# First chunk of the down product: its operands split during the gate/up units, stored as hi and lo, and loaded as whole pages

## The chip, the cores and the metric

One Trainium2 chip, one of its cores. The metric is the device time of one execution in microseconds (us); below, PE, DVE, ACT, POOL and SP are the core's tensor, vector, scalar, GpSimd and sync engines. SP and POOL issue transfers (DMAs).

## The reference, cut to what matters

```python
D_MODEL, SEQ, DEPTH = 1024, 1024, 2
D_FF = ((8 * D_MODEL // 3 + 255) // 256) * 256        # 2816
def swiglu(h, w_gate, w_up, w_down):
    return (jax.nn.silu(h @ w_gate) * (h @ w_up)) @ w_down

def reference(x, ...):
    for i in range(DEPTH):
        h = rms_norm(x, mix_norm[i])
        if i % 2 == 0:
            x = x + short_conv_mixer(h, ...)
        else:
            x = x + dilated_attention_mixer(h, ...)
        h = rms_norm(x, ffn_norm[i])
        x = x + swiglu(h, w_gate[i], w_up[i], w_down[i])
    return rms_norm(x, final_norm)
```

All of it is float32. The change lies in `swiglu`, which runs twice.

## The kernel before, in words

**Products in two parts.** Each float32 operand is split into a high part (ACT copies it to the float32r type) and a low part (DVE subtracts the high part from it). A product is three matmuls: high by high, high by low, low by high (L564 to L566). Weights are split by the helper `split` (lines L139 and L140), activations by `hi` (L556 and L557).

**Winograd.** A product of two by two blocks is made with seven products instead of eight, numbered 1 to 7 and taken in the order 1, 2, 6, 5, 7, 3, 4 (`WINOGRAD`). Of the FFN there are 22 *units*: an even one is a gate, the odd one after it an up of the same two tiles of hidden rows, and the two make a *pair*. From unit 6 on (`SIMPLE`) the products of a pair are interleaved, and products 2 and 4 of a unit are split once more by the same scheme into seven small ones (`DEEPER` + i, 128x256 in PSUM). A step is written (unit, product). DVE combines weights (`combo`), adds up the products in SBUF (`part`, lines L574 and L643, which empty PE's PSUM banks) and multiplies gate by up (L1175). `store` then makes the seven combinations that the down product needs from a pair (`sum`), and POOL stores each to DRAM as `parts[q, m]`, 128x512 (L728, L748), for pair q and product m.

**The down product** takes nine pairs in three chunks of three (`FFN_CHUNK`). For each chunk and each m, `feed` loads three tiles `hin` of 128x512 from `parts` by SP (L763, 256 KB each), and one step later splits them into pages `b`, where a page is 128x1024 and holds high and low side by side: 21 splits per chunk, 126 in all. `down(c, n)` makes the products and adds each result to the residual tile X (L787), which also frees the PSUM bank. The weights of the down product (`raw`, 128x768) and the residual tiles (`x`, loaded back from `spill`) come by the same queue of SP.

**The order of the work.** Each engine takes its instructions in the order in which the code is run. `products` walks the list of steps and calls `filled(n)` in each one, and there the first chunk's feeder makes a step: the first time at (21, `DEEPER`+6), the last small steps of the last unit. So the first chunk's splits lie partly at the end of the units and partly in `down(0, 0)`. A buffer (a `page` or a `half_page`) comes from a pool of slots; the next instruction that writes to a slot waits for the last user of it.

Of the kernel before, what the change touches and what calls it, by code (L numbers as in the profile page):

```python
# [10 lines left out]
F32 = mybir.dt.float32  # L11
F32R = mybir.dt.float32r
# [5 lines left out]
S = 1024  # L18
# [11 lines left out]
WINOGRAD = (1, 2, 6, 5, 7, 3, 4)  # L30
DEEP, DEEPER = (2, 4), 10
SIMPLE = 6
# [63 lines left out]
def trunk(ctx: ExitStack, tc: tile.TileContext, x, gains_in, cwi, ck, cwo, wqkv, wo, relb,  # L96
          wg, wu, wd, oneh, ident, out):
    nc = tc.nc
# [3 lines left out]
    dram = ctx.enter_context(tc.tile_pool(name="dram", bufs=1, space=DRAM))  # L102
    ctx.enter_context(tc.manual_schedule())

    def page(name, dt=F32):
        return pages.tile([128, 1024], dt, name=name, tag="page", bufs=PAGES)
# [3 lines left out]
    def half_page(name, dt=F32):  # L110
        return scope["pool"].tile([128, 512], dt, name=name, tag="half", bufs=scope["halves"])
# [4 lines left out]
    def half(h):  # L116
        return slice(h * HALF, (h + 1) * HALF)
# [11 lines left out]
    def split(src, dst=None, eng=nc.vector):  # L129

        w = src.shape[1]
        if dst is None:
            if w <= HALF:
                t = page("w", F32R)
                dst = t[:, :w], t[:, HALF:HALF + w]
            else:
                dst = page("w_hi", F32R)[:, :w], page("w_lo", F32R)[:, :w]
        hi, lo = dst
        nc.scalar.activation(hi, src, AF.Copy)  # L139
        eng.tensor_tensor(out=lo, in0=src, in1=hi, op=ALU.subtract)  # L140
        return hi, lo
# [4 lines left out]
    ops, made, op_state = [], {}, [0, 0]  # L146
    combos, raw_base, sums_of = {}, {}, {}

    def load_raw(upto):
        while raw_state[0] < min(upto + 1, len(raw_src)):  # L150
            i = raw_state[0]
            raw_tile[i] = page("raw")
            nc.sync.dma_start(raw_tile[i][:, :raw_src[i].shape[1]], raw_src[i])
            raw_state[0] += 1
# [5 lines left out]
    def ensure(upto):  # L160
        while op_state[0] < min(upto + 1, len(ops)):
            key = ops[op_state[0] + 1][0] if op_state[0] + 1 < len(ops) else None
            if key in sums_of:
                sums_of.pop(key)()
            made[op_state[0]] = ops[op_state[0]][1]()
            op_state[0] += 1
# [91 lines left out]
    def unit_order(nu, conv):  # L258

        order = [(0, 1), (1, 1), (0, 2), (1, 2), (2, 1), (2, 2), (3, 1)]  # L260
        if conv:
            order += [(3, 2), (4, 1), (4, 2)] + [(u, m) for m in (6, 7, 5, 4, 3) for u in (0, 1)]
            order += [(2, 6), (2, 5), (2, 7)]
        else:
            order += [(3, 2)] + [(u, m) for m in (6, 7, 4, 5, 3) for u in (0, 1)] + [(2, 6), (2, 5), (2, 7)]
        order += [(3, 6), (2, 4), (2, 3), (3, 5), (3, 7)] + [(4, 1)] * (not conv) + [(3, 4), (3, 3)]
        if not conv:
            for u in range(4, SIMPLE):
                order += [(u, 6), (u, 5), (u, 7), (u + 1, 1), (u, 2), (u, 4), (u, 3)]
            for u in range(SIMPLE, nu, 2):  # L270
                order += [(u, 6), (u, 5), (u, 7), (u + 1, 1), (u, 3), (u + 1, 6), (u + 1, 5), (u + 1, 7)]
                deep = [(u + 1, DEEPER + i) for i in DEEP_ORDER]
                order += deep[:4] + [(u + 1, 3), deep[4]] + [(u + 2, 1)] * (u + 2 < nu) + deep[5:]
            return order
        for u in range(4, nu - 1):
            order += [(u, 6), (u, 5), (u, 7), (u + 1, 1), (u + 1, 2), (u, 4), (u, 3)]
        u = nu - 1
        return order + [(u, m) for m in (6, 5, 7, 4, 3)]
# [86 lines left out]
    def run(*gens):  # L365
        for _ in zip(*gens):
            pass
        for g in gens:
            for _ in g:
                pass  # L370
# [6 lines left out]
    def both(w, ks, acts):  # L377
        banks = two_banks()
        run(product(w, ks, acts, banks))
        return banks  # L380
# [4 lines left out]
    class Norm:  # L385
        def __init__(self, gi):
            self.g = gi
            self.h = {}
            self.acc = self.rstd = None
            self.put_off = None  # L390
            self.by_dma = True
# [140 lines left out]
    class Strassen:  # L532
# [4 lines left out]
        def __init__(self, key, norm, nu, pairs, chunk, tiles, source):  # L537
            self.key, self.norm, self.nu, self.order = key, norm, nu, unit_order(nu, key == CONV)
            self.pairs, self.chunk, self.tiles, self.source = pairs, chunk, tiles, source
            self.b = {m: [None] * 4 for m in range(1, 8)}  # L540
            self.parts = {(q, m): dram.tile([128, HALF], F32, name=f"part_{key}_{q}_{m}")
                          for q in range(pairs) for m in range(1, 8)}
            self.plain = {f: dram.tile([128, S], F32, name=f"plain_{key}_{f}") for f in range(2 * pairs, tiles)}
            self.st, self.quads, self.hid, self.deep, self.sums = {}, {}, {}, {}, []
            self.banks = set()
            self.ahead = 2
            self.slow = ((0, chunk - 1),)

        def page(self, m, k):
            p = page("b", F32R)  # L550
            self.b[m][k] = p[:, :HALF], p[:, HALF:]
            return self.b[m][k]

# [196 lines left out]
        def load_x(self, *ns):  # L750
            for n in ns:
                X[n] = page("x")
                nc.sync.dma_start(X[n], self.source[n])

        def feed(self, c):

            tiles = None
            for m in WINOGRAD + (None,):
                new = None
                if m:  # L760
                    new = [half_page("hin") for k in range(self.chunk)]
                    for k in range(self.chunk):
                        nc.sync.dma_start(new[k], self.parts[c + k, m])  # L763
                if tiles:
                    lows = [self.hi(last, k, t, nc.vector)
                            for k, t in enumerate(tiles)]
                    for lo in lows:
                        lo()
                tiles, last = new, m
                if m:  # L770
                    self.b[m] = [None] * self.chunk
                    yield
# [39 lines left out]
        def run(self, start, hooks={}):  # L812

            self.base = op_state[1]
            last = self.nu - 1

            def filled(n):
                start(n)
                if self.key != CONV:
                    self.now = n + 1  # L820
                    if self.order[n] == (2, 7):
                        prep.append(self.deepen(2))
                    if self.order[n] == (4, 5):
                        prep.append(self.deepen(4))
                    for p in prep:
                        next(p, None)
                    if self.sums and not next(self.sums[0], "done") is None:
                        self.sums.pop(0)
                if self.key == CONV:
                    self.below(n, last)  # L830
                else:
                    if self.order[n][0] == last and n >= self.at(last, DEEPER + 6) - self.base:
                        next(feed, None)
                    if self.order[n] == (last, DEEPER + 7):
                        self.load_x(0, 2)
                        ensure(self.at(last, DEEPER + 4) + 4)
                self.idle(n)

            prep = []
            if self.key == CONV:  # L840
                self.products(filled, hooks)
                self.first_tiles()
                return
            feed = self.feed(0)
            self.products(filled, hooks)
            while self.sums:
                run(self.sums.pop(0))
            for c in range(0, self.pairs, self.chunk):
                self.down(c, 0, feed)
                feed = self.feed(c + self.chunk) if c + self.chunk < self.pairs else self.feed_last()  # L850
                self.down(c, 4, feed)
            run(feed)


    class Conv(Strassen):
# [110 lines left out]
        def step(self, upto):  # L966

            while self.waiting and (upto is None or upto > 0):
                cost = next(self.waiting[0], None)
                if cost is None:  # L970
                    self.waiting.pop(0)
                elif upto is not None:
                    if cost == 0:
                        return
                    upto -= cost
# [907 lines left out]
```

## Time and profile before

| | |
|---|---|
| median of 3 runs | 2172.75 us (2171.66 to 2173.28) |
| the profiled execution | 2172.59 us |
| its span, between first and last instruction | 2170.8 us |
| mean granted clock of PE | 0.993 |
| the two FFNs' units and transitions | about 330 to 777 us, and 1520 to 1954 us |
| one pair of units | 37.34 us |

Rows of the profile read: an instruction's start, its duration, engine, line, operation, the tile written and the tile read; a number behind x joins instructions of one kind in a row, and in brackets stands the engine's idle time before and what ended it. In the table by windows stand, for each stretch, the busy time of each engine with the count of instructions, then the clock that the throttle granted PE (1.00 is full), the mean busy share of the 16 DMA engines, and GB/s.

### The profile page before, as it was taken

Reading aid. Unit: us, or ns where it says so; the run is one execution under the profiler, and the core shown is the slowest. Engines: PE = TensorE matmul, PEld = TensorE weight load, DVE = VectorE, ACT = ScalarE, POOL = GpSimd, SP = SyncE. Lnnn points to the kernel's source line nnn. Section 1 sums busy time; section 2 is a strip of 40 time slices with the busy share of each in tenths; the row PEclk is TensorE's granted clock in tenths of the full one; section 3 lists DMA queues with packets and bytes.
Section 4 is the critical chain, followed back from the end, with each engine's and each line's share of the span. In section 5 each row is a group of like instructions: output and inputs, shape, how many; then the busy total and the mean of one; then the engine's idle time right before and its main releaser. Section 6 shows DMA issues by size and latency. Waiting matters only on the chain.

```text
span 2170.8 us, 30440 instructions
## 1 busy us (share of the span) xinstructions
PE 2131.4 (98%) x11086; PEld 1822.3 (84%) x11086; DVE 1735.0 (80%) x3166; ACT 997.3 (46%) x1792; POOL 172.3 (8%) x224
## 2 busy tenths in 40 slices
PE   8999999999999999999999999999999999999998
PEld 6788877888888878878999999887788888878887
DVE  7798758878888898865777777869988788889886
ACT  7433426444444544445455554535544444454435
POOL 2000001100101000010111111110001001000000
PEclk9999999999999999999999999999999999999999
DMA  7222643313333474323333333544223233365432
GB/s 210 68 93 68 218 146 83 131 69 108 111 107 104 148 266 148 116 61 131 92 92 92 92 92 85 171 127 165 71 88 109 101 108 111 106 235 184 160 93 78
DMA packets 135298, 262.66 MB, mean 121 GB/s; under 512 B 47835, under 2 KB 59115, under 8 KB 135147
## 3 DMA queue, kind: packets, MB, share of 16 engines
q1 hardware_dynamic: 75978, 184.80, 26.6%
q0 software_dynamic: 18000, 52.80, 7.2%
q10 hardware_dynamic: 41168, 23.10, 3.5%
q8 instruction: 88, 1.44, 0.3%
q14 instruction: 64, 0.52, 0.1%
HBM read 187.04 MB, written 66.26 MB: 117 GB/s over the span
## 4 chain that ended last, share of the span: by engine, by line
PE 83%; DVE 8%; ACT 4%; issue 2%; DMA 1%; ACTq 0%; SPq 0%; DVEq 0%
PE bank L564 17%; PE bank L566 17%; PE bank L565 17%; PE bank L362 5%; PE bank L360 5%; PE bank L361 5%; PE bank L1500 4%; PE bank L660 2%; PE bank L659 2%; PE bank L657 2%; PE bank L1428 1%; DVE b L557 1%; PE bank L1427 1%; DVE w L140 1%; DVE x L497 1%
## 5 line engine op out<-in xcount | busy, mean ns | idle before, releaser
L564 PE MATMUL bank<-b,w 128*128 128x512 f32 x1816 | 714.4, 393 | 12.4 <-ACT part L570 6.7
L565 PE MATMUL bank<-b,w 128*128 128x512 f32 x1816 | 711.0, 392 | 0.6 <-DVE b L868 0.6
L566 PE MATMUL bank<-b,w 128*128 128x512 f32 x1816 | 710.2, 391 | 1.1 <-DVE w L140 1.1
L564 PEld LDWEIGHTS bank<-b,w 128*128 128x128 f32 x1816 | 343.6, 189 | 88.1 <-ACT part L570 9.0
L566 PEld LDWEIGHTS bank<-b,w 128*128 128x128 f32 x1816 | 343.0, 189 | 74.0 <-DVE w L140 2.1
L565 PEld LDWEIGHTS bank<-b,w 128*128 128x128 f32 x1816 | 343.6, 189 | 71.5 <-DVE b L868 1.2
L139 ACT ACTIVATE w<-combo 128x512 fp32r<-128x512 f32 (+2 forms) x448 | 229.5, 539 | 266.2 <-DVE combo L187 250.9
L140 DVE TENSOR_TENSOR w<-combo,w 128x512 fp32r<-128x512 f32 (+2 forms) x448 | 254.1, 580 | 44.7 <-ACT w L139 44.3
L570 ACT ACTIVATE part<-bank 128x512 f32<-128x512 f32 x168 | 100.1, 596 | 307.6 <-PE bank L566 303.5
L140 DVE TENSOR_TENSOR w<-raw,w 128x512 fp32r<-128x512 f32 (+2 forms) x312 | 171.6, 568 | 34.4 <-ACT w L139 34.1
L574 DVE TENSOR_TENSOR part<-part,bank 128x256 f32<-128x256 f32 (+1 forms) x328 | 153.9, 497 | 43.5 <-ACT part L570 26.7
L139 ACT ACTIVATE w<-raw 128x512 fp32r<-128x512 f32 (+2 forms) x312 | 151.1, 527 | 45.8 <-PE bank L566 13.4
L787 DVE TENSOR_TENSOR x<-x,bank 128x512 f32<-128x512 f32 x168 | 114.2, 680 | 30.6 <-PE bank L566 30.5
L360 PE MATMUL bank<-w_hi,w 128*128 128x512 f32 (+1 forms) x320 | 120.2, 376 | 1.1 <-ACT w L139 1.1
L362 PE MATMUL bank<-w_hi,w 128*128 128x512 f32 (+1 forms) x320 | 118.7, 371 | 0.7 <-DVE w L140 0.7
L361 PE MATMUL bank<-w_lo,w 128*128 128x512 f32 (+1 forms) x320 | 118.5, 370 | 0.0
L497 DVE TENSOR_TENSOR x<-x,bank 128x512 f32<-128x512 f32 (+1 forms) x104 | 65.9, 641 | 61.0 <-PE bank L362 52.3
L360 PE MATMUL bank<-h_hi,w_hi 128*128 128x512 f32 x256 | 104.6, 408 | 0.3 <-ACT w_hi L139 0.3
L187 DVE TENSOR_TENSOR combo<-raw 128x512 f32<-128x512 f32 (+1 forms) x160 | 102.9, 643 | 0.0
L362 PE MATMUL bank<-h_hi,w_lo 128*128 128x512 f32 x256 | 100.2, 391 | 0.7 <-DVE w_lo L140 0.5
L361 PE MATMUL bank<-h_lo,w_hi 128*128 128x512 f32 x256 | 99.9, 390 | 0.0
L1481 POOL PARTITION_ALL_REDUCE mb<-m x16 | 52.0, 3252 | 422.6 <-DVE m L1478 161.8
(255 smaller groups left out, 3745.9 us busy)
## 6 DMA issues: line engine op xcount, KB each, us to landing
hin<-part SPq DMA_DIRECT2D x126, 256.0 KB
raw<-in_ffn_w_gate SPq DMA_DIRECT2D x44, 512.0 KB
raw<-in_ffn_w_up SPq DMA_DIRECT2D x44, 512.0 KB
part<-sum POOLq DMA_DIRECT2D x72, 256.0 KB, 2.4
raw<-in_ffn_w_down SPq DMA_DIRECT2D x48, 384.0 KB
x<-spill SPq DMA_DIRECT2D x24, 512.0 KB
raw<-in_attn_w_qkv SPq DMA_DIRECT2D x24, 512.0 KB
raw<-in_conv_w_in SPq DMA_DIRECT2D x21, 512.0 KB
```

The lines of the kernel that those rows point to most:

```text
L139: nc.scalar.activation(hi, src, AF.Copy)
L140: eng.tensor_tensor(out=lo, in0=src, in1=hi, op=ALU.subtract)
L187: eng.tensor_tensor(out=c, in0=a, in1=b, op=op)
L360: nc.tensor.matmul(b, whi[:, a], ahi[:, s], start=first, stop=False)
L361: nc.tensor.matmul(b, whi[:, a], alo[:, s], start=False, stop=False)
L362: nc.tensor.matmul(b, wlo[:, a], ahi[:, s], start=False, stop=last)
L564: nc.tensor.matmul(b, hi[:, a], bhi, start=start and k == 0, stop=False, skip_group_check=True)
L565: nc.tensor.matmul(b, hi[:, a], blo, start=False, stop=False, skip_group_check=True)
L566: nc.tensor.matmul(b, lo[:, a], bhi, start=False, stop=k == n - 1, skip_group_check=True)
L570: nc.scalar.activation(t, b, AF.Copy)
L574: nc.vector.tensor_tensor(out=t, in0=t, in1=b, op=ALU.add)
L787: nc.vector.tensor_tensor(out=X[n][:, half(h)], in0=X[n][:, half(h)], in1=b, op=ALU.add)
```

## The change

`early_splits` works in the seven pairs of units 6 to 19. In each it loads three of the 21 tiles `hin`, splits each (the high part into a half page `hi`, the low part in place of `hin`) and stores both by POOL as the two halves of `ready[k, m]` in DRAM. `feed_first` takes the place of `feed(0)`: from step (21, 1) on it loads whole pages `b` of 128x1024 (512 KB) from `ready`, and splits nothing. Chunks two and three stay as they are. Lines below L540 move down: L564 to L566, L574 to L576, L643 to L645, L748 to L750, L787 to L820, L1175 to L1212.

```diff
+            self.ready = {(q, m): dram.tile([128, S], F32, name=f"ready_{key}_{q}_{m}")
+                          for q in range(chunk * (pairs > 0)) for m in range(1, 8)}
...
-            p = page("b", F32R)
+            p = self.pages[m, k] = page("b", F32R)
...
+        def early_splits(self):
+            todo = [(m, k) for m in WINOGRAD for k in range(self.chunk)]
+            loaded = []
+            def load():
+                if todo:
+                    m, k = todo.pop(0)
+                    loaded.append((m, k, half_page("hin")))
+                    nc.sync.dma_start(loaded[-1][2], self.parts[k, m])
+            def made():
+                if loaded:
+                    m, k, t = loaded.pop(0)
+                    parts = half_page("hi", F32R), t.bitcast(F32R)
+                    split(t, parts)
+                    for h, x in enumerate(parts):
+                        nc.gpsimd.dma_start(self.ready[k, m][:, half(h)], x.bitcast(F32))
+            return {(0, 7): (load,), (1, 1): (load,), (0, 3): (made, load), (1, 6): (made,), (1, 5): (made,)}
+
+        def feed_first(self):
+            for m in (1, 0, 2, 0, 6, 0, 0, 5, 0, 7, 0, 0, 3, 4):
+                if m:
+                    self.b[m] = [None] * self.chunk
+                    for k in range(self.chunk):
+                        self.page(m, k)
+                        nc.sync.dma_start(self.pages[m, k].bitcast(F32), self.ready[k, m])
+                yield
...
+                    u, m = self.order[n]
+                    if u >= SIMPLE:
+                        for step in splits.get((u % 2, m), ()):
+                            step()
...
-                    if self.order[n][0] == last and n >= self.at(last, DEEPER + 6) - self.base:
+                    if n >= self.order.index((last, 1)):
                         next(feed, None)
...
-            feed = self.feed(0)
+            feed, splits = self.feed_first(), self.early_splits()
```

PE's instructions and their order are the same. On DVE at the transition (the end of unit 21 and the start of the down product) stood, before:

```order
L1175 TENSOR_TENSOR part<-part 128x512
L557 TENSOR_TENSOR b<-hin,b 128x512 x3
L140 TENSOR_TENSOR w<-raw,w 128x256 x2
L140 TENSOR_TENSOR w<-raw,w 128x384
L574 TENSOR_TENSOR part<-part,bank 128x256 x2
L557 TENSOR_TENSOR b<-hin,b 128x512 x3
L140 TENSOR_TENSOR w<-raw,w 128x384 x2
L187 TENSOR_TENSOR combo<-raw 128x384
```

In the changed kernel the same place reads:

```order
L1212 TENSOR_TENSOR part<-part 128x512
L140 TENSOR_TENSOR w<-raw,w 128x256 x2
L140 TENSOR_TENSOR w<-raw,w 128x384
L576 TENSOR_TENSOR part<-part,bank 128x256 x2
L140 TENSOR_TENSOR w<-raw,w 128x384 x2
L187 TENSOR_TENSOR combo<-raw 128x384
```

The groups of three splits are gone; all else stands in the old order. On DVE in a pair of units (steps (even, 3) and the small steps behind it) stood, before:

```order
L574 TENSOR_TENSOR part<-part,bank 128x512
L140 TENSOR_TENSOR w<-combo,w 128x512
L140 TENSOR_TENSOR w<-raw,w 128x256 x2
L231 TENSOR_TENSOR combo<-combo,raw 128x256 x2
L140 TENSOR_TENSOR w<-raw,w 128x256 x2
```

and now, where `hin<-hin,hi` is the low part of an early split:

```order
L576 TENSOR_TENSOR part<-part,bank 128x512
L140 TENSOR_TENSOR hin<-hin,hi 128x512
L140 TENSOR_TENSOR w<-combo,w 128x512
L140 TENSOR_TENSOR hin<-hin,hi 128x512
L140 TENSOR_TENSOR w<-raw,w 128x256 x2
L231 TENSOR_TENSOR combo<-combo,raw 128x256 x2
L140 TENSOR_TENSOR hin<-hin,hi 128x512
L140 TENSOR_TENSOR w<-raw,w 128x256 x2
```

Three subtractions have come in. On SP's queue at the transition stood, before, after six loads of `hin` for products 1 and 2:

```order
L153 DMA raw<-in_ffn_w_down 128x768 x2
L763 DMA hin<-part_0_6_181 128x512
L763 DMA hin<-part_1_6_188 128x512
L763 DMA hin<-part_2_6_195 128x512
L753 DMA x<-spill_77 128x1024
L753 DMA x<-spill_79 128x1024
L153 DMA raw<-in_ffn_w_down 128x768
```

and now, after six loads of `b` for products 1 and 2:

```order
L153 DMA raw<-in_ffn_w_down 128x768
L785 DMA b<-ready_0_6_244 128x1024
L785 DMA b<-ready_1_6_251 128x1024
L785 DMA b<-ready_2_6_258 128x1024
L785 DMA b<-ready_0_5_243 128x1024
L785 DMA b<-ready_1_5_250 128x1024
L785 DMA b<-ready_2_5_257 128x1024
L153 DMA raw<-in_ffn_w_down 128x768
L785 DMA b<-ready_0_7_245 128x1024
```

The down weights now stand behind whole pages of later products, and the pages of products 3 and 4 behind the first residual tiles.

More of the change, by code (lines that the diff above doesn't have):

```diff
@@ L542, in __init__ @@
                           for q in range(pairs) for m in range(1, 8)}
+            self.ready = {(q, m): dram.tile([128, S], F32, name=f"ready_{key}_{q}_{m}")
+                          for q in range(chunk * (pairs > 0)) for m in range(1, 8)}
             self.plain = {f: dram.tile([128, S], F32, name=f"plain_{key}_{f}") for f in range(2 * pairs, tiles)}
             self.st, self.quads, self.hid, self.deep, self.sums = {}, {}, {}, {}, []
-            self.banks = set()
+            self.banks, self.pages = set(), {}
             self.ahead = 2
```

## The prediction

> **What bounds the kernel now.** I read the page first, its span and its engines.
>
> ```profile
> span 2170.8 us, 30440 instructions
> PE 2131.4 (98%) x11086; PEld 1822.3 (84%) x11086; DVE 1735.0 (80%) x3166; ACT 997.3 (46%) x1792; POOL 172.3 (8%) x224
> ```
>
> PE is busy 98% of the span, so a change that leaves its instructions alone can win only where PE waits or runs at a lower clock. Next I asked for PE's waits at the end of the two FFNs (from 700 to 800 us, then from 1900 to 1970 us; the number after a semaphore is microseconds in all, times, longest). In the stretches of units (440 to 740 and 1610 to 1925 us) that view has no row at all.
>
> ```profile
> PE bank L564 <- ACT b L556: 3.0, 1, 3.0
> PE bank L657 <- DVE part L574: 2.0, 1, 2.0
> ...
> PE bank L657 <- ACT b L556: 2.0, 1, 2.0
> PE bank L564 <- ACT b L556: 1.8, 2, 1.4
> PE bank L564 <- DVE x L787: 0.5, 1, 0.5
> ```
>
> So PE loses 3.0+2.0 = 5.0 us at the first transition from units to the down product and 2.0+1.8+0.5 = 4.3 us at the second: 9.3 us. The table by windows (PE, PEld, DVE, ACT, POOL busy with counts, granted clock, DMA share, GB/s) shows what follows each of them.
>
> ```profile
> 460.00:740.00 280.00, 280.00 (x1512) 243.56 (x1511) 231.40 (x485) 118.83 (x250) 28.03 (x52) 1.00 0.31 104
> 750.00:777.00 27.00, 21.97 (x117) 18.81 (x116) 26.30 (x56) 16.59 (x35) 1.62 (x3) 0.94 0.99 372
> 758.00:760.40 2.40, 0.40 (x4) 0.22 (x3) 2.40 (x7) 1.67 (x3) 0.00 (x0) 1.00 1.02 390
> 769.60:773.00 3.40, 0.56 (x3) 0.14 (x1) 3.37 (x8) 0.93 (x2) 0.34 (x1) 1.00 0.96 348
> 773.03:776.44 3.41, 3.25 (x8) 2.61 (x9) 3.41 (x8) 3.41 (x8) 0.00 (x0) 0.50 1.01 391
> 1933.50:1936.90 3.40, 1.40 (x13) 1.30 (x12) 3.40 (x8) 1.86 (x3) 0.54 (x1) 1.00 1.02 401
> 1936.98:1940.39 3.41, 3.41 (x11) 2.74 (x10) 3.38 (x9) 0.00 (x0) 0.00 (x0) 0.50 1.05 409
> ```
>
> In the units PE is busy all 280 of 280 us. While PE stands at 758 and 770 us, DVE is busy all of 2.40 and 3.37 of 3.40 us: the stalls are DVE's. A window in which PE did 0.56 or 1.40 of 3.40 us is followed by 3.41 us at clock 0.50, each time; the 2.0-us stall at 758 is followed by none. The timeline of DVE there has no idle time from 756.21 to 773.4 (eight of its rows, with three of PE's):
>
> ```profile
> 756.21 0.69 DVE L1175 TENSOR_TENSOR part<-part 128x512 f32<-128x512 f32 x1
> 756.81 1.89 DVE L557 TENSOR_TENSOR b<-hin,b 128x512 fp32r<-128x512 f32 x3
> 758.62 1.22 DVE L140 TENSOR_TENSOR w<-raw,w 128x256 fp32r<-128x256 f32 x3
> 759.76 0.74 DVE L574 TENSOR_TENSOR part<-part,bank 128x256 f32<-128x256 f32 x2
> 760.42 1.89 DVE L557 TENSOR_TENSOR b<-hin,b 128x512 fp32r<-128x512 f32 x3
> ...
> 765.35 1.89 DVE L557 TENSOR_TENSOR b<-hin,b 128x512 fp32r<-128x512 f32 x3
> ...
> 769.03 1.89 DVE L557 TENSOR_TENSOR b<-hin,b 128x512 fp32r<-128x512 f32 x3
> ...
> 772.36 0.68 DVE L787 TENSOR_TENSOR x<-x,bank 128x512 f32<-128x512 f32 x1
> ...
> 760.32 0.35 PE L657 MATMUL bank<-t,w 128*128 128x256 f32 x1 [2.00 <-DVE part L574]
> ...
> 769.78 0.39 PE L566 MATMUL bank<-b,w 128*128 128x512 f32 x1
> 773.19 0.77 PE L564 MATMUL bank<-b,w 128*128 128x512 f32 x1 [3.02 <-ACT b L556]
> ```
>
> PE's 760.32 starts 0.15 us after the first of the two adds of 759.76 ends (0.41 us each by the group row below); 773.19 starts 0.15 us after L787 of 772.36 ends (0.68), since that add frees its bank. The "ACT" of that row had been done long before. Four groups of three splits stand in this chain, 1.81 us each (756.81 to 758.62).
>
> **The change, part by part.**
>
> *Splits leave the transition.* First stall: one group stands ahead of the late add. Without it L574 starts 759.76−1.81 = 757.95, ends 758.36, PE goes on at 758.51, 0.19 us after its free time 760.32−2.00 = 758.32. Second stall: four groups, 7.2 us, leave the chain, so L787 ends at 773.04−7.2 = 765.8; PE, itself 1.8 earlier, wants the bank at about 768.4. That wait goes, with 2.6 us to spare, and with it the clock window. The second FFN has the same rows in the same order, so I cost it alike: 9.3 us of waits, less 2×0.2. A window at 0.50 does in 3.41 us what takes half of it at full clock: 2×1.7 = 3.4 us, or 3.25/2+3.41/2 = 3.3 by the PE time in the rows. Later groups of the first chunk go from the down product too, where PE has no wait: nothing.
>
> A page of the Trainium skill speaks against the 3.3: "TensorE: Matmul & The Clock Gate", section "What's actually happening", has the clock halved only after at least one idle window, free-running and 3.4 us long. The trace agrees on the length (3.41 us) and not on the condition, since 1.40 us of PE work stood in 1933.50:1936.90 ahead of a 0.50 row; by the page the sum would lack these 3.3 us.
>
> *Splits enter the units.* Three per pair, 14 pairs. Their prices, and the units' rows they fall among (592 to 602 us):
>
> ```profile
> L557 DVE TENSOR_TENSOR b<-hin,b 128x512 fp32r<-128x512 f32 x126 | 79.2, 682 | 0.0
> L574 DVE TENSOR_TENSOR part<-part,bank 128x256 f32<-128x256 f32 x224 | 83.1, 411 | 0.0
> ...
> 592.68 1.33 ACT L139 ACTIVATE w<-raw 128x256 fp32r<-128x256 f32 x4
> ...
> 591.37 0.69 DVE L140 TENSOR_TENSOR w<-combo,w 128x512 fp32r<-128x512 f32 x1 [1.22 <-ACT w L139]
> 593.12 0.76 DVE L140 TENSOR_TENSOR w<-raw,w 128x256 fp32r<-128x256 f32 x2 [1.06 <-ACT w L139]
> ...
> 598.25 0.69 DVE L643 TENSOR_TENSOR c<-part,bank 128x512 f32<-128x512 f32 x1 [1.02 <-ACT part L570]
> ...
> 600.86 0.74 DVE L574 TENSOR_TENSOR part<-part,bank 128x256 f32<-128x256 f32 x2
> ...
> 601.74 0.28 PE L657 MATMUL bank<-t,w 128*128 128x256 f32 x1
> ```
>
> In a row of three they take 0.60 us each (1.81/3): 1.8 us of DVE per pair, as much of ACT, which is 46% busy. The first falls into DVE's wait of 1.22 us. The second comes ahead of 593.12 and holds ACT's four copies of 592.68 back by one copy, some 0.5 us, so that DVE's splits of w stand 0.8 us later, at 593.92; the third adds 0.6: 1.4 us late, and the wait of 1.02 us ahead of 598.25 takes all of it but 0.4. So L574 ends at 600.86+0.41+0.4 = 601.67 at worst, and PE follows 0.15 us behind, 601.8 against 601.74. That is the edge: 0.05 us. Bounds for a pair: no less than nothing, since PE has no wait there to lose; no more than 1.8−0.3 = 1.5 us, all the added DVE time less the 601.74−601.27−0.15 = 0.3 us that PE has in hand. I take 0.1 per pair, near the lower end because the row it is worked out from says 0.05, and a few waits more stand in the way: 14×0.1 = 1.4 us.
>
> *Stores and early loads.* Six stores more per pair on POOL (8% busy), three loads on SP.
>
> ```profile
> hin<-part SPq DMA_DIRECT2D x126, 256.0 KB
> part<-sum POOLq DMA_DIRECT2D x72, 256.0 KB, 2.4
> ...
> 616.17 1.14 POOL L728 DMA_DIRECT2D part<-part  x2 [15.67 <-DVE part L1175]
> ...
> 616.40 0.68 DVE L736 TENSOR_TENSOR sum<-c,part 128x512 f32<-128x512 f32 x1
> 617.00 0.68 DVE L736 TENSOR_TENSOR sum<-part 128x512 f32<-128x512 f32 x1
> ...
> 740.68 9.96 SPq L763 DMA_DIRECT2D hin<-part  x6
> ...
> 730.00:740.00 10.00, 10.00 (x46) 8.27 (x45) 5.71 (x10) 3.32 (x6) 0.00 (x0) 1.00 0.20 66
> ```
>
> Nine transfers of 256 KB in a pair's 37.3 us are 63 GB/s on top of 104, where 372 to 409 have been seen: nothing, with some 200 in hand. A store lands 2.4 us after its issue; the half page of the third split's hi is wanted again about 598.25, its copy is done by some 594.5, so 1 us is left there; if stores took 4 us, DVE would wait for them (below). The queued gate loads behind the three hin loads on SP go out when PE has done with their pages, so the loads ahead cost nothing.
>
> While POOL issues from 616.17 to 617.31, DVE's adds start 0.60 us apart (616.40, 617.00), as everywhere. The Trainium skill, "GPSIMD Engine Reference", section "1. Specifications", has POOL share its SBUF interfaces with VectorE, in contention with DVE instructions of two SBUF inputs, as these are. If each issue held DVE for its 0.57 us, the sum would have 6×14×0.57 = 48 us against it; by the row it is nothing, and a transfer's issue is no POOL arithmetic.
>
> *Whole pages come in.* 21 pages of 512 KB take the place of 21 halves, on a DMA path that is full from 750 to 777 (share 0.99). The six of m=1 and 2 go out, by when their pages come free, from about 730 us (an estimate), in a stretch where the DMA share is 0.20, ahead of where the halves went (740.68). The other 15 need 7.9 MB. Before, 372 GB/s × 27 us = 10.0 MB landed in 750:777, 3.9 of it hin (15×0.26). So 6.1+7.9 and two down weights of 0.4 each, moved behind the first pages, make 14.8 MB from 741 on: 38 us at 390 GB/s, to 779 in place of 777. Last to land are m=4 and the x pages; by their uses on PE, now 6.7 us earlier, I work out 1 to 4 us of margin. Cost bounds: nothing, to 3 us and a clock window in each FFN; I take nothing, since the third down weight, first in need (PE about 761.7), lands about 758.
>
> **Sum.** −9.3 −3.3 +0.4 +1.4 = −10.8 us. The profiled execution took 2172.6 us (1.8 around its span), 0.1 under the median of the runs shown: 2172.6−10.8 = 2161.8.
>
> **The rivals.** *Late pages.* If the DMA path brings 300 GB/s rather than 390, the third weight lands about 762 and the x pages some 10 us later than the sum above: one stall of 1.5 to 3 us in each FFN, and about half of the clock windows again: 2×2.3 = 4.6 us back, 2166.4. For it: the full path. Against: its row shows 390 and more. It turns the sign only from 6 us per FFN on.
>
> *Units held (the slower side).* The add that empties PE's bank (L574 at 600.86) comes late in each pair by more than PE's 0.3 us, because the 0.4 above is joined by a late store whose half page L643 waits for. The gain without the units' term is 12.2 us, so it decides at 12.2/14 = 0.87 us per pair and shows as slower from 16.5/14 = 1.18. At its bound of 1.5: 21.0−12.2 = +8.8, 2181.4. For it: the edge of 0.05 us, 14 times. Against: at 606 us DVE waits again, so a delay doesn't carry over.
>
> *Clock windows stay.* By the page named, short stalls aren't what halves the clock; then the 0.50 rows come from elsewhere and stay: 2161.8+3.3 = 2165.1. Against: two rows, each right behind a half-idle window.
>
> *PE isn't freed.* DVE keeps its place but stands for weights or x pages that land late, in the very 2 and 3 us that the splits held: about 2172, no change.
>
> **How the numbers follow.** Forecast 0.64 (2158 to 2165), late pages 0.16 (2165 to 2169), units held 0.10 (0.07 of it slower, 0.03 no change), windows 0.03, not freed 0.07 (0.04 no change, 0.02 faster, 0.01 slower). About 0.2%, 4.3 us, is what can be told from no change: faster 0.64+0.16+0.03+0.02 = 0.85, same 0.07, slower 0.08. The range takes the forecast and late pages with the clock windows, 2158 to 2169; its low end is the sum without the units' term and the 0.4, and 2 us for PE's restarts that the wait rows don't count.
>
> **What would show it.** Right: no PE wait at 758 and 770 nor in the second FFN's transition, no 0.50 row there, PE's waits in the units near none, DVE with gaps in the transition. Late pages: PE or DVE waits on `b<-ready`, raw or x loads. Units held: PE waits for L576 (the old L574) once per pair. What would make it wrong above all is that edge: 0.05 us worked out from one pair, used for fourteen.

## The result, and the profile after

The changed kernel takes 2162.1 us (2159.1 to 2162.3, 4 runs) against 2172.2 us before, a ratio of 0.9948 (95% interval 0.9937 to 0.9960). In five further runs it took 2161.6 us, 0.9952 (0.9939 to 0.9964). The profiled execution took 2161.95 us. Its page begins:

```profile
span 2159.9 us, 30731 instructions
## 1 busy us (share of the span) xinstructions
PE 2128.0 (99%) x11086; PEld 1819.9 (84%) x11086; DVE 1735.9 (80%) x3166; ACT 996.4 (46%) x1792; POOL 217.7 (10%) x308
```

PE has the same 11086 matmuls. DVE and ACT are as busy as before: no work was saved, it was moved. PE's waits at the two transitions (700 to 800, 1890 to 1970 us) have shrunk to one row each:

```profile
PE bank L659 <- DVE part L576: 0.2, 1, 0.2
...
PE bank L659 <- DVE part L576: 0.2, 1, 0.2
```

The table by windows for the transitions and for the units:

```profile
750.00:777.00 27.00, 26.74 (x149) 23.02 (x148) 23.88 (x54) 9.13 (x21) 2.17 (x4) 1.00 1.03 415
1919.00:1947.00 28.00, 27.80 (x157) 24.16 (x156) 24.80 (x55) 9.46 (x23) 2.17 (x4) 1.00 1.03 416
460.00:740.00 280.00, 280.00 (x1510) 243.62 (x1509) 243.57 (x507) 129.04 (x271) 50.87 (x94) 1.00 0.50 170
```

PE is busy 26.74 of 27.00 us where it was 21.97, at a clock of 1.00 where it was 0.94. In the units DVE went from 231.40 to 243.57 us of 280 and the DMA share from 0.31 to 0.50, with PE busy all 280. A part of the price stands in the second FFN's units (1610 to 1925 us), which had no row before (the view leaves out waits of 0.15 us and less):

```profile
PE bank L659 <- ACT w L139: 0.9, 1, 0.9
```

Setting the starts of the same matmul side by side in the two traces gives the balance. The changed kernel starts 0.6 us late within the first 55 us, before anything of the change has run; it loses 0.4 us in the first FFN's units, gains 6.2 at the first transition and 0.7 between the FFNs, loses 1.6 in the second FFN's units and gains 6.3 at the second transition. With 0.1 lost after that it ends 10.5 us earlier. Before 330 us all kernels of this document run the same code, and yet their profiles lie up to 3.0 us apart there (1.6 us behind the kernel before in a repeat of the changed kernel, 1.4 us ahead of it in the run with two halves more), with two or three windows at clock 0.50. So medians that differ by 1 or 2 us don't rank these kernels; where such a difference matters below, it is read from the starts of the same matmuls.

The new DVE chain at the first transition, with ACT's row that it stands for:

```profile
757.79 1.22 DVE L140 TENSOR_TENSOR w<-raw,w 128x256 fp32r<-128x256 f32 x3
758.93 0.74 DVE L576 TENSOR_TENSOR part<-part,bank 128x256 f32<-128x256 f32 x2
762.08 1.03 DVE L140 TENSOR_TENSOR w<-raw,w 128x384 fp32r<-128x384 f32 x2 [2.41 <-ACT w L139]
...
768.62 0.68 DVE L820 TENSOR_TENSOR x<-x,bank 128x512 f32<-128x512 f32 x1
...
761.52 1.35 ACT L139 ACTIVATE w<-raw 128x384 fp32r<-128x384 f32 x3 [7.93 <-DMA raw<-in_ffn_w_down]
```

DVE now has idle time, 2.41 us, and what it stands for is a down weight (`raw`) that lands at 761.5.

### The profile page after: what moved, and what is told of

The parts are those of the page before. It is cut to its first block, busy times and chain, and to the rows that moved or that the text cites. A ratio compares the mean times of both kernels' runs of the same rounds, so it can differ in the third digit from the quotient of the medians.

```text
span 2159.9 us, 30731 instructions
## 1 busy us (share of the span) xinstructions
PE 2128.0 (99%) x11086; PEld 1819.9 (84%) x11086; DVE 1735.9 (80%) x3166; ACT 996.4 (46%) x1792; POOL 217.7 (10%) x308
## 4 chain that ended last, share of the span: by engine, by line
PE 86%; DVE 6%; ACT 4%; issue 2%; DMA 2%; ACTq 0%; SPq 0%; DVEq 0%
PE bank L566 18%; PE bank L567 18%; PE bank L568 18%; PE bank L362 5%; PE bank L360 5%; PE bank L361 5%; PE bank L1537 4%; PE bank L659 2%; PE bank L662 2%; PE bank L661 2%; PE bank L1465 1%; PE bank L1464 1%; PE bank L1405 1%; PE bank L1404 1%; PE bank L1403 1%
## 5 line engine op out<-in xcount | busy, mean ns | idle before, releaser
L566 PE MATMUL bank<-b,w 128*128 128x512 f32 x1816 | 712.6, 392 | 7.5 <-ACT part L572 6.7
L566 PEld LDWEIGHTS bank<-b,w 128*128 128x128 f32 x1816 | 342.7, 189 | 82.3 <-ACT part L572 9.0
L576 DVE TENSOR_TENSOR part<-part,bank 128x256 f32<-128x256 f32 (+1 forms) x328 | 154.2, 500 | 40.0 <-ACT part L572 26.7
L820 DVE TENSOR_TENSOR x<-x,bank 128x512 f32<-128x512 f32 x168 | 114.8, 684 | 37.4 <-PE bank L568 33.6
```

What stands on the lines that cost most here:

```text
L566: nc.tensor.matmul(b, hi[:, a], bhi, start=start and k == 0, stop=False, skip_group_check=True)
L576: nc.vector.tensor_tensor(out=t, in0=t, in1=b, op=ALU.add)
L820: nc.vector.tensor_tensor(out=X[n][:, half(h)], in0=X[n][:, half(h)], in1=b, op=ALU.add)
```

## Where the gain comes from

**The two halves apart.** First the units' part alone: the first chunk is fed as before.

```diff
-            feed, splits = self.feed_first(), self.early_splits()
+            feed, splits = self.feed(0), self.early_splits()
...
-                    if n >= self.order.index((last, 1)):
+                    if self.order[n][0] == last and n >= self.at(last, DEEPER + 6) - self.base:
```

> Early loads, splits and stores in the seven pairs as in the changed kernel, but the first chunk is fed as before, so that its operands are split a second time at the transition and the stored parts are not read. My account: no gain is left, the units' loss stays: 2172.7 + 0.4 to 2 us = 2173 to 2175, PE's waits of 2 and 3 us stand at the transitions as before. Rival (early work slows the units by 0.1 us a pair or more, hidden in the result of the whole by a larger gain): 2176 or more.

Measured: 2173.5 us, 1.0007 (0.9998 to 1.0016), so +1.2 us against 2172.3, which the interval does not separate from no change. At the first transition PE waits as it did before the change:

```profile
PE bank L566 <- ACT b L558: 3.0, 1, 3.0
PE bank L659 <- DVE part L576: 2.0, 1, 2.0
```

Then the transition's part alone:

```diff
-            feed, splits = self.feed_first(), self.early_splits()
+            feed, splits = self.feed_first(), {}
...
-                        nc.sync.dma_start(self.pages[m, k].bitcast(F32), self.ready[k, m])
+                        nc.sync.dma_start(self.pages[m, k].bitcast(F32), self.source[k])
```

> No early loads, splits or stores; the pages of the first chunk are loaded from the residual stream in DRAM instead (same size, the first chunk's products are of other values). My account: the whole gain of the transitions without the units' loss, 2172.5 - 12.6 = 2160, and no wait of PE in the units. Rival (the units' loss is larger than 2 us): 2158 or less.

Measured: 2160.0 us, 0.9943 (0.9930 to 0.9957), with no wait in the units. By the medians the transitions are worth 12.3 us, and the units take 1.6 to 2.1 us of that back (2161.6 and 2162.1 less 2160.0). By the starts of the same matmuls it is 12.9 us and, for the two profiles of the changed kernel, 1.9 and 2.3 us.

**Is it DVE?** The change takes the splits' copies off ACT too, and replaces late halves by early pages. So DVE's time alone was put back, in `feed_first`:

```diff
-            for m in (1, 0, 2, 0, 6, 0, 0, 5, 0, 7, 0, 0, 3, 4):
+            for n, m in enumerate((1, 0, 2, 0, 6, 0, 0, 5, 0, 7, 0, 0, 3, 4, 0, 0)):
+                if n in range(9, 16):
+                    t = half_page("dummy")
+                    for k in range(self.chunk):
+                        a, b = (self.pages[1, k][:, half(h)].bitcast(F32) for h in range(2))
+                        nc.vector.tensor_tensor(out=t, in0=a, in1=b, op=ALU.subtract)
```

> The changed kernel with seven groups of three subtractions of 128x512 put back on DVE at the places where the splits stood (their results are not used); ACT has none of its copies, and the pages are loaded whole as in the changed kernel. My account (DVE's chain alone made the stalls): waits of about 2 and 3 us at the first transition and of 2 and 2 us at the second come back, with two windows at clock 0.50: 2173 to 2175. Rival (ACT's copies, or the late landing of the halves, made them): 2162 to 2164.

Measured: 2177.2 us, 1.0020 (1.0011 to 1.0029). PE's waits at the first transition and one of the groups:

```profile
PE bank L566 <- ACT w L139: 2.4, 2, 2.1
PE bank L659 <- DVE part L576: 2.2, 1, 2.2
...
756.86 2.13 DVE L785 TENSOR_TENSOR dummy<-b 128x512 f32<-128x512 f32 x3
```

Both waits are back, without ACT's copies and with the pages as early as in the changed kernel: DVE's queue made them. It came out 2 us above what I expected: a group takes 2.05 us (756.86 to 758.91) where the splits took 1.81, and there are four windows at clock 0.50 at the transitions (near 762, 775, 1939 and 1953 us) in place of two.

**Which group makes which wait?** The same with `if n in (9,)`, the first group only.

> The changed kernel with only the first of the seven groups of three subtractions put back on DVE (results not used; 2.05 us a group as measured with all seven). My account (four groups stand ahead of the second stall's add, one ahead of the first's): the wait of 2.2 us comes back at the start of each transition, the second wait does not, since its add ends 3 x 2.05 us earlier than with seven groups, some 4 us before PE wants the bank: 2161.8 + 2 x 2.0 = 2166, up to 2169 if each wait is followed by a window at clock 0.50. Rival (the two waits hang together, the first one bringing on the second): 2172 or more.

Measured: 2166.6 us, 0.9971 (0.9960 to 0.9983). The waits at the first and the second transition:

```profile
PE bank L659 <- ACT w L139: 2.3, 1, 2.3
...
PE bank L659 <- DVE part L576: 2.3, 1, 2.3
```

One group brings back the first wait of each transition and not the second. The two waits are separate debts of one chain, as the prediction had them.

**How many groups must go?** Early splits for products 1, 2, 6, 5 and 7 alone; the rest as before, from halves.

```diff
-            todo = [(m, k) for m in WINOGRAD for k in range(self.chunk)]
+            todo = [(m, k) for m in WINOGRAD[:5] for k in range(self.chunk)]
...
-            for m in (1, 0, 2, 0, 6, 0, 0, 5, 0, 7, 0, 0, 3, 4):
+            for m in (1, 0, 2, 0, 6, 0, 0, 5, 0, 7, 0, 0, 0):
...
+            for new, old in ((3, 0), (4, 0), (0, 3), (0, 4)):
+                if new:
+                    tiles[new] = [half_page("hin") for k in range(self.chunk)]
+                    for k in range(self.chunk):
+                        nc.sync.dma_start(tiles[new][k], self.parts[k, new])
+                if old:
+                    self.b[old] = [None] * self.chunk
+                    lows = [self.hi(old, k, t, nc.vector) for k, t in enumerate(tiles[old])]
+                    for lo in lows:
+                        lo()
+                yield
```

> Only the operands of products 1, 2, 6, 5 and 7 are split early (five pairs of units per FFN, 60 stores in place of 84); those of products 3 and 4 are loaded as halves and split in the down product, as before. My account (only groups ahead of the add that frees the bank at the second stall count): the transitions are as free as with all seven, 2161 to 2162.5. Rival (DVE has no room for the last two groups either): waits at L820's adds, 2164 or more.

Measured: 2161.2 us, 0.9949 (0.9936 to 0.9963), with waits of 0.2 us at the transitions, and 0.9 us once in the second FFN's units. The last two groups stood where DVE had time; moving them buys nothing.

## What the units pay for

The wait of 0.9 us in the second FFN was 1.0 us in the second profile of the same kernel, in the same pair of units; the first row is the changed kernel's profile, the second the repeat's (1790 to 1820 us).

> The changed kernel once more. My account (splits out of DVE's chain at the transition gain 12.6 us of span; the units give back 0.4 us in small pieces and 1.1 us by one store that landed late): 2162, with a wait of PE of 0.9 us by no means in the same pair each time, perhaps in none. Rival (the units' loss is a fixed cost of each pair): the same 0.9 us wait at the same pair again, and no other.

```profile
PE bank L659 <- ACT w L139: 0.9, 1, 0.9
...
PE bank L659 <- ACT w L139: 1.0, 1, 1.0
```

The repeat has a wait of 0.2 us more, in the first FFN's fifth pair. So the 0.9 us is no accident of one execution; in this the rival stood in the right. The rows of the changed kernel lead back from it (all within 1799 to 1810 us):

```profile
1799.18 8.65 SPq L153 DMA_DIRECT2D raw<-in_ffn_w_gate  x2
...
1799.36 0.54 POOL L774 DMA_DIRECT2D ready<-hin  x1 [0.18 <-issue]
...
1806.03 0.60 ACT L572 ACTIVATE part<-bank 128x512 f32<-128x512 f32 x1 [3.34 <-PE bank L662]
...
1809.27 0.75 DVE L576 TENSOR_TENSOR part<-part,bank 128x256 f32<-128x256 f32 x2
```

PE goes on when the first add of 1809.27 ends; the ACT named in its wait had been done since 1807.2. That add is late because DVE stood for ACT's save of 1806.03, and this is where the label misleads again: the bank it saves was ready at 1804.6. The save writes to the slot that held the first split's low part, and waits until that part's store, issued at 1799.36, has landed: 6.6 us later, at 1805.93. In the other thirteen pairs the same store took 4.6 to 5.1 us and the save started on time, with 0.2 to 0.65 us to spare. The view of the stores (L774) gives the range, and the list of issues the medians (a store from POOL took 2.4 us before the change):

```profile
DMA to landing us min/median/max: 2.4/4.1/6.6
...
ready<-hi POOLq DMA_DIRECT2D x42, 256.0 KB, 4.1
ready<-hin POOLq DMA_DIRECT2D x42, 256.0 KB, 4.3
part<-sum POOLq DMA_DIRECT2D x72, 256.0 KB, 3.5
```

The store of 1799.36 has the pair's gate load of 512 KB right ahead of it (SP, 1799.18). In the run below that works one product earlier no load is issued beside the same store, and it takes 2.3 us in the median pair.

**Without the stores:**

```diff
-                    for h, x in enumerate(parts):
-                        nc.gpsimd.dma_start(self.ready[k, m][:, half(h)], x.bitcast(F32))
...
-                        nc.sync.dma_start(self.pages[m, k].bitcast(F32), self.ready[k, m])
+                        nc.sync.dma_start(self.pages[m, k].bitcast(F32), self.source[k])
```

> The changed kernel without the 84 stores; the pages are loaded from the residual stream in DRAM instead (the first chunk's products are of other values); early loads and splits stay. My account (the units' loss is a save on ACT that waits for a store to land): no wait of PE in the units, 2160.0 to 2160.6. Rival (the loss is DVE's added 1.8 us a pair): 2161.5 to 2162, with the wait of 1 us still in the second FFN's fifth pair.

Measured: 2160.4 us, 0.9941 (0.9929 to 0.9953), no wait in the units of either FFN: the wait of 0.9 us is the stores'. It is not the whole of the loss. Beside the kernel before, PE falls back by 0.05 to 0.06 us in each of the fourteen pairs, at one and the same matmul, which is too little for the view of waits. In the pair whose rows the prediction used it is the matmul of 603.00, that of 601.74 in the kernel before:

```profile
602.43 0.74 DVE L576 TENSOR_TENSOR part<-part,bank 128x256 f32<-128x256 f32 x2
...
603.00 0.35 PE L659 MATMUL bank<-t,w 128*128 128x256 f32 x1
603.18 0.28 PE L661 MATMUL bank<-t,w 128*128 128x256 f32 x1
```

The first of the two adds ends at 602.84 (0.41 us each), and PE's matmul follows 0.16 us behind it. It now takes 0.35 us in place of 0.28, and the next one starts 0.18 us after it in place of 0.12: a loss of 0.06 us, and this is the edge of the prediction. With no early splits at all (the transition's part alone) the pairs lose nothing. The table adds up, by the starts of the same matmuls, what each profile gained on the kernel before in the units (440 to 745 and 1610 to 1925 us) and in the transitions (745 to 800 and 1925 to 1975 us); the last two runs follow below.

| profile | units | transitions |
|---|---|---|
| transition's part alone | 0.0 us | +12.9 us |
| without the stores | -0.8 us | +12.5 us |
| the changed kernel | -1.9 us | +12.8 us |
| the changed kernel again | -2.3 us | +13.1 us |
| splits in reverse order | -2.3 us | +13.2 us |
| five products, the fifth pair left out | -0.5 us | +12.7 us |

So the early splits cost 0.8 us (fourteen times the small edge), and the late store 1.1 us in one profile and 1.5 in the other.

**One product earlier:**

```diff
-            return {(0, 7): (load,), (1, 1): (load,), (0, 3): (made, load), (1, 6): (made,), (1, 5): (made,)}
+            return {(0, 5): (load,), (0, 7): (load,), (1, 1): (made, load), (0, 3): (made,), (1, 6): (made,)}
```

> The changed kernel with each pair's loads and splits one product (2.7 us) earlier, so that the first split's stores are out before the pair's gate load is issued. My account: the first split's store of the low part lands before that load starts, the wait of 1 us in the fifth pair goes, 2160.2 to 2161.0. Rival (buffers are handed on in another order and another instruction waits for a store): 2162 or more, with waits of PE in most pairs.

Measured: 2162.3 us, 0.9953 (0.9940 to 0.9965). The wait near 1809 is gone, and one of 0.6 us has come in the first FFN's units (at 529 us). ACT's row ahead of it names its cause, a store again, of a `sum`, into whose slot the second split's copy goes; from that copy on, DVE works without a pause from 521.63 to the late add of 528.86:

```profile
PE bank L659 <- ACT w L139: 0.6, 1, 0.6
...
520.96 0.63 ACT L139 ACTIVATE hi<-hin 128x512 fp32r<-128x512 f32 x1 [0.68 <-DMA part<-sum]
```

My expectation failed here, the rival held in kind, though in one pair and not in most: a shift changes who inherits which slot.

**Why that pair?** Other tiles are stored in it when the splits go in the reverse order (`WINOGRAD[::-1]`):

> The changed kernel with the early splits in the reverse order of products (4, 3, 7, 5, 6, 2, 1), so that the fifth pair stores product 6 and the third pair product 7. If the late store belongs to the fifth pair (what is read beside it): the wait of about 1 us stays in the fifth pair of the second FFN, near 1810. If it belongs to the place of product 7's stores in DRAM: it moves to the third pair, near 1735. 2161 to 2162.5 either way.

Measured: 2159.6 us, 0.9943 (0.9929 to 0.9957), below the expected range, though not separated from the changed kernel; by the table its units lose no less. The wait stayed, 1.1 us, in the fifth pair:

```profile
1808.27 0.36 PE L659 MATMUL bank<-t,w 128*128 128x256 f32 x1 [1.11 <-ACT w L139]
```

So the late store belongs to the pair and not to the place that is written. The trace tells more of that pair. It holds sixteen updates of a store's semaphore, as many as there are DMA engines. Fifteen updates of the store of 1799.36 had come after 4.64 us, as in the other pairs; the sixteenth came at 6.57. Meanwhile another queue, of the kind that the profile calls `instruction`, made one transfer of 16 KB, from 1803.67 to 1804.63 (the changed kernel, 1799.3 to 1806 us; kind, packets, MB, share of the engines):

```profile
q0 software_dynamic: 461, 1.52, 59.1%
q1 hardware_dynamic: 144, 0.52, 31.0%
q8 instruction: 1, 0.02, 0.9%
```

It comes there in the repeat and in this run too, with the sixteenth update at 6.67 and 6.75 us and the fifteenth at 4.77 and 4.57. In the first FFN's fifth pair of the changed kernel it starts 4.4 us after the store's issue, when that store has all but landed, and the stores behind it lose 1 us; no other pair has one so near. The run one product earlier shows the same: such a transfer starts at 518.60, and the `sum` store of 516.32, for which ACT's copy of 520.96 waits, has fifteen updates after 2.62 us and the last after 4.62. No run moves this transfer, so that it is the cause is read from the traces and not tested, and of the 2 us by which the last part is late its 0.96 us explains a half.

**The pair left out.** The run with five products, its fifteen splits in pairs one to four and six:

```diff
-                    if u >= SIMPLE:
+                    if u >= SIMPLE and u // 2 != 7:
```

> Fifteen early splits as in the run with products 1, 2, 6, 5 and 7 alone, in pairs one to four and six, the fifth pair left out. If the late store belongs to the fifth pair: no wait over 0.3 us in the units, 2159.5 to 2160.8, the lowest so far. Otherwise 2161 to 2162.

Measured: 2159.3 us, 0.9943 (0.9930 to 0.9955), no wait of PE in the units of either FFN:

```profile
460.00:740.00 280.00, 280.00 (x1511) 243.58 (x1510) 239.51 (x498) 125.95 (x265) 43.74 (x82) 1.00 0.46 153
1634.00:1906.00 272.00, 272.00 (x1476) 236.94 (x1475) 232.86 (x487) 124.45 (x261) 43.12 (x80) 1.00 0.46 153
```

This has the whole gain of the transitions, with fewer stores, and by the table its units lose 0.5 us, where the five products with the fifth pair in use lost 1.8, counted alike. Its median is below that of the changed kernel and of the run with five products, though the intervals overlap.

## How thin the transfers' cover is

The six pages of products 5 and 7 loaded twice:

```diff
-                        nc.sync.dma_start(self.pages[m, k].bitcast(F32), self.ready[k, m])
+                        for n in range(1 + (m in (5, 7))):
+                            nc.sync.dma_start(self.pages[m, k].bitcast(F32), self.ready[k, m])
```

> The changed kernel with the six pages of products 5 and 7 loaded twice in each FFN: 3.1 MB more ahead of the pages of products 3 and 4 and of the residual tiles, 7.6 us at the 415 GB/s that the transition shows. My account (the transition's loads are hidden with 1 to 4 us to spare): 4 to 7 us of waits in each FFN, 2169 to 2176. Rival (more than 8 us to spare): 2162.

Measured: 2205.4 us, 1.0153 (1.0137 to 1.0169), far beyond both accounts. It measured another thing than I had meant. PE's wait, and SP's own at the first transition:

```profile
PE bank L566 <- ACT w L139: 19.7, 1, 19.7
...
SPq L786 <- DMA b<-ready: 26.6, 6, 5.0
```

The second load of a page waits on SP until the first has landed, six times, 26.6 us in all, and the down weight behind them waits with it. The DMA share fell to 0.68 meanwhile, so this says nothing of the transfers' cover. A cleaner question: two loads of 256 KB more into free half pages, ahead of the third down weight.

```diff
+                if m == 7:
+                    for k in range(2):
+                        nc.sync.dma_start(half_page("spare"), self.parts[k, 1])
```

> The changed kernel with two loads of 256 KB more per FFN, into spare half pages, on SP right ahead of the third down weight. At the 415 GB/s seen in the transition they take 1.26 us. My account (in the changed kernel that weight lands at 761.5, ACT stands for it, PE wants the product of its split at 763.06 and the freed bank 0.2 us before it comes): it lands at 762.7, PE waits about 0.3 us for the split and 1.2 us for the bank, 1.5 us per FFN: 2161.8 + 3.0 = 2164.8. Rival (the transfers have 1 to 4 us to spare, as I forecast): 2161.5 to 2162.5, no more PE wait than 0.2 us.

Measured: 2165.3 us, 0.9966 (0.9953 to 0.9978). PE's waits at the two transitions, beside the 0.2 us each that were there:

```profile
PE bank L566 <- ACT w L139: 1.3, 2, 0.7
...
PE bank L566 <- ACT w L139: 2.0, 2, 1.3
```

Half a megabyte costs 1.3 and 2.0 us of waits, and by the starts of the same matmuls the two transitions gain 8.4 us in place of 12.8: in the changed kernel the down weights have next to nothing to spare.

## Why the prediction was right, and where it was not

*Splits leave the transition.* Right in mechanism and size. 12.2 us were forecast for the two (9.3 + 3.3 − 0.4); the run with the transition alone gained 12.3 by its median and 12.9 by the starts of its matmuls. The first wait's rest was forecast at 0.19 us and is 0.2. Both windows at clock 0.50 have gone.

*The second wait.* The term came out, its working did not. The add L787 was to end at 765.8, 2.6 us ahead of PE. It ends at about 769.3 (its row of 768.62, as L820), 0.2 us late: PE's next matmul on that bank starts at 769.40 where it could have started at 769.18. The cause is in the DMA step: the third weight was to land "about 758", from 390 GB/s over the whole backlog. Between 740 and 750 us the changed kernel moved less:

```profile
740.00:750.00 10.00, 10.00 (x54) 8.64 (x54) 6.67 (x17) 4.80 (x12) 0.00 (x0) 1.00 0.94 324
```

It landed at 761.5, and DVE stood 2.41 us for its split. The changed kernel is 1.0 us late at that point; without the two, the add would have ended at 765.9, as forecast. The lower rate of 740 to 750 us is 0.7 MB less, or 1.6 us at 415 GB/s, so it explains the larger part, and not all, of the 2.5 us that are left of the weight's delay (761.5 less 758 and less 1.0). This is the rival of late pages at the very point where it begins to cost. I gave that rival 0.16; the run with two halves more shows that it needed only half a megabyte.

*Splits enter the units.* 1.4 us were forecast, as fourteen losses of 0.1; the changed kernel lost 1.9 and 2.3 us there, of another make. The 0.05 us of the DVE chain, the part that I distrusted, was right in every pair: 0.8 us in fourteen, with the stores and without. The 0.1 that I took in its place had no row to it, and that it came near the whole is luck. The term that was mis-sized is the store, which I put at nothing and which cost 1.1 to 1.5 us. I took 2.4 us from stores that went out alone, and the tightest user to be L643; with a gate load ahead it took 4.6 to 6.6, and the tightest user was ACT's save. This is the rival of held units by its own mechanism, a late store, in one pair of seven and not in all. In the sum of 2161.8 these errors nearly cancel: the transitions gave 0.6 to 0.9 us more than forecast, and the units took 0.5 to 0.9 us more.

*Clock windows.* That they would stay (0.03) is refuted. The run with one group gives the rule more closely: the same wait of 2.3 us at both transitions, once followed by 0.50 and once not. The rows are pairs of one window and the next:

```profile
757.96:761.37 3.41, 1.24 (x10) 1.27 (x11) 3.41 (x9) 1.35 (x3) 0.00 (x0) 1.00 1.02 417
761.37:764.78 3.41, 3.41 (x11) 2.77 (x10) 3.38 (x9) 1.56 (x3) 0.00 (x0) 0.50 1.03 418
1928.72:1932.13 3.41, 1.75 (x15) 1.55 (x13) 3.34 (x7) 0.19 (x1) 0.54 (x1) 1.00 1.02 412
1932.13:1935.54 3.41, 2.82 (x18) 2.63 (x19) 3.38 (x9) 1.17 (x3) 0.00 (x0) 1.00 1.03 421
```

With PE busy 1.24 us of a window the clock fell in the next, with 1.75 it did not; before the change 1.40 was too little. In five profiles (before, the units' part alone, seven groups and one group put back, two halves more) the transitions have nine windows at full clock with 0.5 to 1.42 us of PE work, each followed by 0.50, and seven with 1.74 to 2.5, none of them followed by it. What the Trainium skill ("TensorE: Matmul & The Clock Gate", section "What's actually happening") says of a free-running window of 3.4 us agrees; that a whole window must be idle does not.

*DVE beside POOL's issues.* Had each of POOL's issues held DVE, that would have cost 48 us. The trace does not bear that out: for the same 3166 instructions DVE is busy 1735.9 us where it was 1735.0, and the changed kernel's row of its largest group of splits has a mean of 581 ns, with 308 instructions on POOL; before it was 580 with 224. What the Trainium skill ("GPSIMD Engine Reference", section "1. Specifications") says of SBUF interfaces that POOL shares with VectorE shows no cost here.

```profile
L140 DVE TENSOR_TENSOR w<-combo,w 128x512 fp32r<-128x512 f32 (+2 forms) x448 | 254.7, 581 | 27.5 <-ACT w L139 27.1
```

## What to carry to other kernels

Where one engine is full for a few microseconds and has idle time in a long stretch ahead, moving its work there pays just for what stands ahead of the late result: here five groups of seven gave all of the gain. A margin of 0.05 us that was worked out from the rows of one pair held in all fourteen, so take such a number as it stands and multiply it. Price a moved step by its buffers too: who inherits each slot, and how long its store takes with the transfers that are issued beside it, and not with those that it had to itself. In a wait that names an engine long done, look for a transfer into or out of the slot being written.

## What the runs showed that I had not expected

A store of 256 KB that took 2.3 to 2.4 us alone took 4.6 to 5.1 us with a load of 512 KB issued 0.2 us ahead of it on another queue. It took 6.6 us in one pair, the same in each profile of the changed kernel, with one of sixteen parts 2 us behind the rest and a 16 KB transfer of the kind `instruction` beside it. A second load into a page whose first load is under way held the whole queue of SP, up to 5.0 us a load. And an equal wait of PE cost a slow-clock window of 3.41 us or none, by how much work it left PE in the window where it fell.
